# Seven half products for eight in the values and gates of two heads, and pauses moved behind the first eight pairs

## The chip, the core and the metric

The kernel runs on one core of a Trainium2 chip. The metric is the device time of one execution in microseconds (us). The kernel before takes 2068.49 us (median of 3 runs, 2067.83 to 2068.57).

## The reference, cut to what matters

Two layers over 256 tokens of 2048 columns, all in float32. Layer 0 is a gated linear attention with four heads, layer 1 a sliding-window attention, and each is followed by a squared-relu MLP of width 8192. The change touches two places: the values `v` and the gates `r` of the linear attention, and the order of the work in both MLPs.

```
u = rmsnorm(h, norm_mix[0])
proj = u @ w_in                       # (256, 2048) @ (2048, 6160)
q, k, v, r, glr = split(proj)         # v and r: 2048 columns each, 512 per head
o = gated_linear_attention(q, k, v, log_sigmoid(glr @ w_g2 + b_g) / 16)   # per head
o = rmsnorm(o, g_o) * silu(r)         # per head
h = h + o @ w_o
h = h + relu(rmsnorm(h, norm_mlp[0]) @ w1) ** 2 @ w2
```

## The kernel before

**Matmuls in two parts.** No operand is used as it is: each float32 matrix is split into a high part (rounded to the fast matmul type, `F32R`) and a low part (the rest), and a product is made of three matmuls, high x high, high x low and low x high. Weights come in tiles of 512 x 512 (four k-blocks of 128 rows, 1 MB) by a DMA of the SP queue. `halve` (line 104) splits one such tile in two halves: ScalarE (ACT) casts the high part (`wh`, line 116), VectorE (DVE) subtracts it for the low part (`wl`, line 117). `ws` and `wl` have three buffers, `wh` has four half buffers.

**Heads.** For each of the four heads, `gemm_mov` (line 138) is run twice over the four weight tiles of a column block of 512: once for the values (evacuated by `evac_v`, line 568) and once for the gates (`evac_r`, line 573, with the silu). The activations `act0` (16 k-blocks, high and low) stand still in the array and 512 weight columns move: per tile 4 k-blocks x 2 halves of the tokens x 3 parts = 24 matmuls of 512 columns, so 192 per head. The activations carry the norm's weight but not its factor `rstd`, which comes in at the evacuation. `mix_head` (line 562) joins a head's values and gates two to three ticks later, with a few full float32 matmuls and transposes on the tensor engine (PE).

**MLPs.** Each MLP runs four groups `g` (line 823). A group makes four wide products with `w1` (`gemm_wide`, line 192) and then multiplies their squared relu with a slab of `w2`: in `seven` (line 714, Strassen-Winograd on 2 x 2 half blocks in seven half products) for two column pairs, or, in the last group of the second MLP, by four more wide products. A wide product works in pairs: one matmul of 512 columns (high weights times high and low activations) and one of 256 (low weights times high), 16 pairs per weight tile and 64 per product, 256 per group. In its first tile the pairs of the first two of its four PSUM banks come first (the first eight pairs), then those of the other two.

**Pauses.** `pause` (line 678) issues two matmuls of one column each into a bank of tag `ms`; what they compute is not used. The first group of each MLP has two of them (at ticks 9 and 13 of the MLP), every later group one ahead of its first wide product, and the last wide stage of the second MLP one.

**Order of the work.** A helper `later(n, fn)` calls `fn` at the n-th `tick` from now; `gemm_mov`, `gemm_wide` and `seven` tick once for each half weight tile. Behind that, the framework orders the instructions of each engine when the kernel is built: by priority (the order of the program, with a head start for weight loads and splits), each as soon as its operands and buffers are free by the framework's own reckoning; an instruction that is not ready is passed by the next one that is. On the chip every engine then works through its list in that order. PSUM has eight banks: four of tag `acc`, two `tp`, two `ms`.

Of the kernel before, what the change touches and what calls it, by code (L numbers as in the profile page):

```python
# [16 lines left out]
P = 128  # L17
T = 256
NT = T // P
D = 2048  # L20
KT = D // P
C = 512
# [4 lines left out]
DV = 512  # L27
# [6 lines left out]
WS = 3  # L34
WHL = 4
WPRI = 60
# [4 lines left out]
RS = 4  # L41
# [7 lines left out]
def yoco_kernel(ctx: ExitStack, tc: tile.TileContext, x, norms, mlp_w1, mlp_w2, a_w_in, w_glr, w_gate, a_g_o, a_w_o,  # L49
                kv_w_k, kv_w_v, kv_g_k, b_w_q, b_g_q, b_sinks, b_w_o, out):  # L50
    nc = tc.nc
# [3 lines left out]
    actp = ctx.enter_context(tc.tile_pool(name="actp", bufs=8))  # L55
    wp = ctx.enter_context(tc.tile_pool(name="wp", bufs=2))
# [5 lines left out]
    def bank(shape, tag, dtype=F32):  # L62
        return ps[tag].tile(shape, dtype, name=tag, tag=tag)
# [29 lines left out]
    G_MIX0, G_MIX1, G_MLP0, G_MLP1, G_KV = (gT[:, KT * i:KT * (i + 1)] for i in range(5))  # L93
# [10 lines left out]
    def halve(ws, o=C, n=2, between=None):  # L104

        whs = [wp.tile([P, 2, C], F32R, name="wh", tag="wh", bufs=WHL) for _ in range(2)]
        wl = wp.tile([P, 4, C], F32R, name="wl", tag="wl", bufs=WS)
        with tc.high_priority(offset=WPRI):
            for k in range(0, 4, n):
                wh = whs[k // 2]  # L110
                js, ks = slice(k % 2, k % 2 + n), slice(k, k + n)
                with ExitStack() as order:
                    if between:
                        for ins in between(k):
                            order.enter_context(tc.issue_after(ins.ins))
                    h = nc.scalar.copy(out=wh[:, js, :o], in_=ws[:, ks, :o])  # L116
                    l = nc.vector.tensor_sub(out=wl[:, ks, :o], in0=ws[:, ks, :o], in1=wh.bitcast(F32)[:, js, :o])  # L117
                if between:
                    last[:] = h, l
        return [(whs[k // 2][:, k % 2], wl[:, k]) for k in range(4)]  # L120
# [14 lines left out]
    def piece(w, col, n=C):  # L135
        return lambda kq: [w[kq * C:(kq + 1) * C, col:col + n]]

    def gemm_mov(src, act, evac, step=4):

        accs = []  # L140

        def run(kq):
            if kq == 0:
                accs.extend(bank([P, C], "acc") for _ in range(NT))
            halves = split_w(src(kq), step)
            ah, al, _ = act[kq]
            for k in range(4):
                wh, wl = halves[k]
                for t in reversed(range(NT)):
                    tt = slice(t * P, (t + 1) * P)  # L150
                    st, sp = kq == 0 and k == 0, kq == 3 and k == 3
                    mm(accs[t], ah[:, k, tt], wh, st, False, skip_group_check=True)
                    mm(accs[t], ah[:, k, tt], wl, False, False, skip_group_check=True)
                    mm(accs[t], al[:, k, tt], wh, False, sp, skip_group_check=True)
                if k == 1:
                    tick()
            tick()
            if kq == 3:
                for t in reversed(range(NT)):
                    evac(t, accs[t])  # L160
        return run
# [128 lines left out]
    rb = sm.tile([P, T], F32, name="rb", tag="rb")  # L290
    ga = ExitStack()
    gp = ga.enter_context(tc.tile_pool(name="gp", bufs=1))
    ss = gp.tile([P, 2, T], F32, name="ss")
    rbq = gp.tile([P, T], F32, name="rbq")
    rb4, rbq4 = (a.rearrange("p (o t n) -> p o t n", o=1, t=NT).broadcast_to([P, 2, NT, P]) for a in (rb, rbq))
    sqx = []

# [31 lines left out]
    g2 = ga.enter_context(tc.tile_pool(name="g2", bufs=2))  # L329


    cum = gp.tile([P, NT, P], F32, name="cum")
    nc.gpsimd.memset(cum, 1.0 / TAU)
    for t, sign in enumerate((1, -1)):
        nc.gpsimd.affine_select(out=cum[:, t], in_=cum[:, t], compare_op=ALU.is_ge, fill=0.0, base=0,
# [13 lines left out]
    go = gp.tile([P, DV], F32, name="go")  # L349
# [181 lines left out]
    def mix(h, t, act):  # L531
# [25 lines left out]

        later(MX, flip)

    acto = [None] * H  # L560

    def mix_head(h, t):
# [4 lines left out]
    for h in range(H):  # L567
        def evac_v(t, acc, h=h):
            v = g2.tile([P, DV], F32, name="v", tag="v", bufs=4)
            nc.scalar.activation(out=v, in_=acc, func=AF.Copy, scale=rstd[:, t:t + 1])  # L570
            vs[h, t] = v

        def evac_r(t, acc, h=h):
            g = g2.tile([P, DV], F32, name="g", tag="g", bufs=4)
            nc.scalar.activation(out=g, in_=acc, func=AF.Silu, scale=rstd[:, t:t + 1])
            nc.gpsimd.tensor_mul(out=g, in0=g, in1=go)
            gs[h, t] = g

        go_all(gemm_mov(piece(w_in, 2048 + h * C), act0, evac_v))
        go_all(gemm_mov(piece(w_in, 4096 + h * C), act0, evac_r))  # L580
        for t in range(NT):
            later(2 + t, lambda h=h, t=t: mix_head(h, t))

# [83 lines left out]
    def mlp(w1, w2, act, r, gains):  # L667
# [155 lines left out]
        for g in range(4):  # L823
            w = w2[g * D:(g + 1) * D]
            seven_of = 0 if g == 3 and not gains else 2
            us, op, uf = {}, None, {}
            if g:
                pause()
            else:
                for n in (RS + 5, RS + 9):  # L830
                    later(n, pause)
            for c in range(NC4):
                if c >= seven_of:
                    us[c] = new_act()
# [24 lines left out]
                go_all(gemm_wide(piece(w1, g * D + c * C), act, evac_u))  # L859
            if seven_of:  # L860
                for n in range(2):
                    seven(w, n, op, us, g, g == 3 or (g == 2 and not gains), acts, gains if g == 3 else (), sq, nr)
                continue
            pause()
            for c in range(NC4):
                def evac_x(f, acc, c=c):
                    d = xt[c][:, f]
                    for u in (1, 0):
                        nc.vector.tensor_add(out=d, in0=acc[:, u], in1=d)
                    r = c * C + f * P  # L870
# [242 lines left out]
```

## Time and profile before

| | |
|---|---|
| median of 3 runs | 2068.49 us |
| the profiled execution | 2068.05 us, its span 2066.3 us |
| PE busy | 2053.9 us (99% of the span), 10778 matmuls |
| PE weight loads busy | 1743.0 us (84%) |
| DVE busy | 1429.5 us (69%) |
| ACT busy | 1151.7 us (56%) |
| GpSimd (POOL) busy | 159.0 us (8%) |
| granted PE clock, mean | 0.999 of full speed |
| HBM read | 406.71 MB, 198 GB/s over the span |

One execution was recorded by the hardware profiler. Busy time is the union of an engine's instructions; the records of matmuls overlap, since they are pipelined and their ends are modelled, so the pace of PE is read from the starts of its instructions or from their number in a stretch. Times of a row are us from the start of the span, durations of one instruction in ns where they say mean. An arrow `out<-in` names the tiles, `L117` is line 117 of the kernel.

### The profile page before, as it was taken

What the parts mean: (1) busy time and instruction counts of PE and PEld (TensorE: products, weight loads), DVE (VectorE), ACT (ScalarE), POOL (GpSimd) and SP (SyncE); (2) the same over time, 40 slices, a digit from 0 to 9 for tenths busy, and PEclk for the clock granted to TensorE, in tenths of its full rate; (3) what the DMA queues carried; (4) which work ended last, traced back from release to release, by engine and by line L of the source; (5) the groups of instructions that cost most, each with busy time, mean ns of one, the idle gap of its engine ahead of it and who ended that gap; (6) DMA issues with size and microseconds to landing.
All of it is one profiled execution on the core that took longest, in us unless ns stands there. A gap on an engine that the chain in (4) does not pass through costs nothing.

```text
span 2066.3 us, 27059 instructions
## 1 busy us (share of the span) xinstructions
PE 2053.9 (99%) x10778; PEld 1743.0 (84%) x10778; DVE 1429.5 (69%) x1632; ACT 1151.7 (56%) x1560; POOL 159.0 (8%) x171
## 2 busy tenths in 40 slices
PE   9999999999999999999999999999999999999999
PEld 9998888888888888888887877788888888888888
DVE  6686444567866886786798677666876786797554
ACT  6745445555555555554566677555655554655543
POOL 2252111000000000000001121000000000000000
PEclk9999999999999999999999999999999999999999
DMA  7445554755875785686676443655785776586653
GB/s 281 143 143 169 178 183 164 243 183 176 257 232 185 219 264 189 197 259 213 183 214 186 164 142 123 231 177 190 223 261 188 219 241 210 180 237 192 198 183 128
DMA packets 210654, 410.55 MB, mean 199 GB/s; under 512 B 7024, under 2 KB 15232, under 8 KB 210528
## 3 DMA queue, kind: packets, MB, share of 16 engines
q1 hardware_dynamic: 194704, 377.51, 53.9%
q0 software_dynamic: 15104, 30.23, 8.4%
q8 instruction: 84, 1.38, 0.3%
q10 hardware_dynamic: 720, 1.09, 0.2%
q14 instruction: 42, 0.34, 0.0%
HBM read 406.71 MB, written 2.10 MB: 198 GB/s over the span
## 4 chain that ended last, share of the span: by engine, by line
PE 94%; DVE 3%; ACT 2%; issue 1%; DMA 1%; POOL 0%; SPq 0%; ACTq 0%; DVEq 0%; POOLq 0%
PE acc L80 57%; PE ms L80 21%; PE tp L80 14%; ACT sc L1006 1%; DVE wl L117 1%; PE tp L606 1%; ACT wh L116 1%; DVE sc L1011 0%; PE tp L939 0%; DMA ws<-in_a_w_in_dram 0%; DVE st L1000 0%; DMA xt<-in_x_dram 0%; PE tp L555 0%; DVE po L1028 0%; DVE act L238 0%
## 5 line engine op out<-in xcount | busy, mean ns | idle before, releaser
L117 DVE TENSOR_TENSOR wl<-ws,wh 128x1024 fp32r<-128x1024 f32 (+1 forms) x636 | 778.8, 1232 | 455.4 <-ACT wh L116 453.2
L116 ACT CAST wh<-ws 128x1024 fp32r<-128x1024 f32 (+1 forms) x636 | 659.1, 1040 | 564.1 <-PE acc L80 372.1
L80 PE MATMUL acc<-wh,act 128*128 128x512 f32 x1792 | 574.5, 394 | 0.2 <-ACT act L237 0.2
L80 PE MATMUL acc<-act,wh 128*128 128x512 f32 (+1 forms) x1664 | 505.9, 365 | 2.1 <-ACT wh L116 1.3
L80 PEld LDWEIGHTS acc<-wh,act 128*128 128x128 f32 x1792 | 335.6, 188 | 72.4 <-issue 2.0
L80 PE MATMUL acc<-act,wl 128*128 128x256 f32 x1408 | 394.9, 281 | 0.2 <-DVE wl L117 0.2
L80 PE MATMUL acc<-wl,act 128*128 128x512 f32 x896 | 349.0, 390 | 0.0
L80 PEld LDWEIGHTS acc<-act,wh 128*128 128x128 f32 x1664 | 298.1, 190 | 54.2 <-ACT wh L116 1.5
L80 PEld LDWEIGHTS acc<-act,wl 128*128 128x128 f32 x1408 | 267.2, 190 | 1.4 <-DVE wl L117 0.5
L80 PE MATMUL tp<-act,wh 128*128 128x512 f32 x592 | 232.4, 397 | 0.0
L80 PE MATMUL ms<-act,wh 128*128 128x512 f32 x576 | 228.6, 397 | 0.0
L80 PEld LDWEIGHTS acc<-wl,act 128*128 128x128 f32 x896 | 168.4, 188 | 34.4 <-issue 1.7
L117 DVE TENSOR_TENSOR wl<-wx,wh 128x1024 fp32r<-128x1024 f32 x112 | 134.9, 1222 | 65.5 <-ACT wh L116 64.0
L116 ACT CAST wh<-wx 128x1024 fp32r<-128x1024 f32 x112 | 117.2, 1053 | 99.4 <-PE acc L80 42.3
L80 PE MATMUL ms<-act,wl 128*128 128x256 f32 x576 | 161.4, 280 | 0.0
L80 PE MATMUL tp<-act,wl 128*128 128x256 f32 x576 | 161.1, 280 | 0.0
L80 PE MATMUL ms<-wh,act 128*128 128x512 f32 x448 | 142.7, 390 | 0.0
L80 PEld LDWEIGHTS tp<-act,wh 128*128 128x128 f32 x592 | 111.1, 188 | 26.9
L80 PEld LDWEIGHTS ms<-act,wh 128*128 128x128 f32 x576 | 108.1, 188 | 26.3
L732 POOL DMA_DIRECT2D wx<-in_mlp_w_dram x28 | 36.1, 1290 | 1118.8 <-DVE wl L117 1017.8
L80 PEld LDWEIGHTS ms<-act,wl 128*128 128x128 f32 x576 | 108.7, 189 | 0.0
L80 PEld LDWEIGHTS tp<-act,wl 128*128 128x128 f32 x576 | 108.7, 189 | 0.0
(233 smaller groups left out, 2238.6 us busy)
## 6 DMA issues: line engine op xcount, KB each, us to landing
ws<-in_mlp_w_dram SPq DMA_DIRECT2D x228, 1024.0 KB, 5.2
ws<-in_a_w_in_dram SPq DMA_DIRECT2D x44, 1024.0 KB, 5.0
wx<-in_mlp_w_dram POOLq DMA_DIRECT2D x28, 1024.0 KB, 9.3
ws<-in_a_w_o_dram SPq DMA_DIRECT2D x16, 1024.0 KB, 4.9
ws<-in_b_w_q_dram SPq DMA_DIRECT2D x16, 1024.0 KB, 5.0
ws<-in_b_w_o_dram SPq DMA_DIRECT2D x16, 1024.0 KB, 5.0
wx<-in_mlp_w_dram SPq DMA_DIRECT2D x14, 1024.0 KB, 5.1
wy<-in_mlp_w_dram SPq DMA_DIRECT2D x14, 1024.0 KB, 8.0
```

The lines of the kernel that those rows point to most:

```text
L80: nc.tensor.matmul(o, lhsT=l, rhs=r, start=start, stop=stop, **kw)
L116: h = nc.scalar.copy(out=wh[:, js, :o], in_=ws[:, ks, :o])
L117: l = nc.vector.tensor_sub(out=wl[:, ks, :o], in0=ws[:, ks, :o], in1=wh.bitcast(F32)[:, js, :o])
L606: nc.tensor.transpose(out=tp[:, j, t], in_=xs[c][:, t, (2 * b + j) * P:(2 * b + j + 1) * P], identity=ident)
L732: nc.gpsimd.dma_start(out=ws, in_=block(i, j).rearrange("(k p) n -> p k n", p=P), accum_op=ALU.add)
L1006: nc.scalar.activation(out=sc[:, h], in_=sc[:, h], func=AF.Exp, bias=nmx[:, h:h + 1], scale=f[:, h:h + 1], accum_out=su[:, h:h + 1])
```

## The change

In heads 2 and 3 the eight weight tiles (four for the values, four for the gates) are no longer taken as eight products with both halves of the tokens. The upper two k-tiles of 512 rows and the two column blocks (values, gates) form a 2 x 2 matrix of weight tiles, the two token halves and the two k-tiles a 2 x 2 matrix of activations, and `seven_vr` makes their product in seven half products of 12 matmuls; the two other k-tiles are multiplied as before (`plain`, four times 24 matmuls). For this

- `normed` makes, during head 1, activations that carry the whole norm (`rstd` too), splits them anew, and makes four combinations of the two first k-tiles with their own high and low parts;
- the weight combinations are made in `wx` (a pair of half tiles): GpSimd starts two DMAs that add a tile on top of it in memory (`accum_op`), and DVE adds a tile to `b12` and to `wx`;
- `wx` has one half in `wx0`, whose memory `ss`, `rbq` and `cum` have used before, and one in a buffer of tag `mlev`; a fourth combination lives in `wgh`, the third in the other `mlev` buffer;
- the evacuations are adds, subtractions and copies, with the silu on top.

In the MLPs the second pause of the first group goes, and every other one is called at the first tick of its first wide product (behind the first eight pairs), not ahead of it.

```diff
+    def normed(b, *cs):
+        bs = slice(2 * b, 2 * b + 2)
+        us = []
+        for c in cs:
+            if b == 0:
+                xh[c] = new_act()
+            u = g2.tile([P, 2, T], F32, name="xu", tag="oh")
+            for j in range(2):
+                kt = 2 * b + j
+                nc.vector.scalar_tensor_tensor(out=u[:, j], in0=xt[c][:, kt], scalar=G_MIX0[:, c * 4 + kt:c * 4 + kt + 1],
+                                               in1=rb, op0=ALU.mult, op1=ALU.mult)
+            ah, al, _ = xh[c]
+            nc.scalar.copy(out=ah[:, bs], in_=u)
+            nc.vector.tensor_sub(out=al[:, bs], in0=u, in1=ah.bitcast(F32)[:, bs])
+            us.append(u)
+        if cs[0]:
+            return
...
+        ua, ub = us
+        es, sf = (g2.tile([P, 2, 2, P], F32, name="xe", tag="ol") for _ in range(2))
+        sub = lambda o, i, j: nc.vector.tensor_sub(out=o, in0=i, in1=j)
+        sub(es[:, 0], ua[:, :, P:], ub[:, :, P:])
+        sub(es[:, 1], ua[:, :, :P], es[:, 0])
+        sub(sf[:, 0], ub[:, :, :P], es[:, 1])
+        sub(sf[:, 1], ua[:, :, :P], ua[:, :, P:])
+        for o, e in zip(comb["es"], (es[:, 0], es[:, 1], sf[:, 0], sf[:, 1])):
+            nc.scalar.copy(out=o[:, 0, bs], in_=e)
+            sub(o[:, 1, bs], e, o.bitcast(F32)[:, 0, bs])
+
+    def seven_vr(h):
...
+        def load_x(i, j, queue=nc.gpsimd, **kw):
+            with tc.high_priority(offset=WPRI):
+                for n in range(2):
+                    queue.dma_start(out=wx[n], in_=block(i, j)[:, 2 * n:2 * n + 2], **kw)
...
+        def product(b, o, ws):
+            p, st = use(b)
+            halves = halve(ws)
+            for k in range(4):
+                wh, wl = halves[k]
+                mm(p, o[0][:, k], wh, st and k == 0, False, skip_group_check=True)
+                mm(p, o[0][:, k], wl, False, False, skip_group_check=True)
+                mm(p, o[1][:, k], wh, False, k == 3, skip_group_check=True)
+            tick()
+            return p
...
+        wx = [wx0, g2.tile([P, 2, C], F32, name="wx1", tag="mlev")]
+        load_x(0, 0, nc.sync)
+        p = product("A", token(0, 0), wx)
+        load_x(0, 1, accum_op=ALU.add)
+        nc.scalar.mul(out=v, in_=p, mul=-1.0)
+        plain(2, 1, "E", "F")
+        y = load(1, 1)
+        product("E", s4, y)
+        b12 = load(0, 1)
+        with tc.high_priority(offset=WPRI):
+            nc.vector.tensor_add(out=b12, in0=b12, in1=y)
+        p = product("C", e7, b12)
+        nc.scalar.copy(out=x22, in_=p)
+        plain(3, 1, "E", "F")
+        p = product("D", e5, wx)
+        load_x(1, 1, accum_op=ALU.add)
+        nc.scalar.copy(out=x21, in_=p)
+        plain(2, 0, "A", "C")
+        plain(3, 0, "A", "C")
+        add(v, product("D", s2, wx), v)
+        add(x12, banks["E"], v)
+        silu(x12)
+        sub(x22, v, x22)
+        add(x22, banks["F"], x22)
+        silu(x22)
+        sub(x21, x21, v)
+        b21 = load(1, 0)
+        with tc.high_priority(offset=WPRI):
+            for n in range(2):
+                nc.vector.tensor_add(out=wx[n], in0=wx[n], in1=b21[:, 2 * n:2 * n + 2])
+        product("A", token(1, 0), b21)
+        nc.scalar.copy(out=x11, in_=banks["A"])
+        add(x21, product("C", token(1, 1), wx), x21)
...
-        go_all(gemm_mov(piece(w_in, 2048 + h * C), act0, evac_v))
-        go_all(gemm_mov(piece(w_in, 4096 + h * C), act0, evac_r))
+        if h < 2:
+            if h == 2 - 1:
+                for n, fn in ((6, (0, 0, 1)), (8, (1, 0, 1)), (11, (0, 2)), (12, (1, 2)), (13, (0, 3)), (14, (1, 3))):
+                    later(n, lambda fn=fn: normed(*fn))
+            go_all(gemm_mov(piece(w_in, 2048 + h * C), act0, evac_v))
+            go_all(gemm_mov(piece(w_in, 4096 + h * C), act0, evac_r))
+        else:
+            seven_vr(h)
...
-            if g:
-                pause()
-            else:
-                for n in (RS + 5, RS + 9):
-                    later(n, pause)
+            later(1 if g else RS + 5, pause)
...
-            pause()
+            later(1, pause)
```

## Rows read from the trace of the kernel before

**Rows 1.** The page: PE's busy time, its granted clock, the chain by engine.
```profile
PE 2053.9 (99%) x10778; PEld 1743.0 (84%) x10778; DVE 1429.5 (69%) x1632; ACT 1151.7 (56%) x1560; POOL 159.0 (8%) x171
...
PEclk9999999999999999999999999999999999999999
...
PE 94%; DVE 3%; ACT 2%; issue 1%; DMA 1%; POOL 0%; SPq 0%; ACTq 0%; DVEq 0%; POOLq 0%
```

**Rows 2.** Stretches, heads then `seven`: us, each engine's busy us, PEclk, DMA share, GB/s.
```profile
198.00:218.00 20.00, 20.00 (x90) 16.57 (x89) 9.27 (x8) 8.64 (x9) 0.00 (x0) 1.00 0.58 183
...
510.00:550.80 40.80, 40.80 (x181) 33.76 (x180) 35.67 (x36) 25.58 (x29) 1.29 (x1) 1.00 0.80 240
```

**Rows 3.** Line 575, gate evacuation, two per head: duration, first and last start.
```profile
L575 ACT ACTIVATE g<-acc,rstd x8: 683/690/692, 175.3 to 319.8; 128x512 f32<-128x512 f32 x8
```

**Rows 4.** Lines of 222 to 265 us, in the heads: the weight split on DVE.
```profile
L117 DVE TENSOR_TENSOR wl<-ws,wh 128x1024 fp32r<-128x1024 f32 x15 | 19.0, 1268 | 22.8 <-ACT wh L116 22.8
```

**Rows 5.** Lines of the whole span by form: DVE operations, count, busy us, mean ns.
```profile
L803 DVE TENSOR_TENSOR wy<-wy,ws 128x2048 f32<-128x2048 f32 x14 | 32.0, 2287 | 0.1
...
L238 DVE SCALAR_TENSOR_TENSOR act<-tp,gT,act 128x256 fp32r<-128x256 f32 x64 | 30.0, 480 | 9.4 <-ACT act L237 9.2
L846 DVE TENSOR_TENSOR m<-acc,m 128x256 f32<-128x256 f32 x64 | 24.7, 423 | 0.0
L855 DVE TENSOR_TENSOR act<-u,act 128x512 fp32r<-128x512 f32 x36 | 24.4, 683 | 0.0
...
L544 DVE SCALAR_TENSOR_TENSOR og<-ms,ov,g 128x512 f32<-128x512 f32 x8 | 6.0, 751 | 5.7 <-POOL ov L245 5.7
```

**Rows 6.** DVE in order of time while GpSimd works on levels beside it: start, us.
```profile
148.00 2.06 DVE L117 TENSOR_TENSOR wl<-ws,wh 128x1024 fp32r<-128x1024 f32 x1
```

**Rows 7.** DMA issues: KB each, median us to landing.
```profile
wx<-in_mlp_w_dram POOLq DMA_DIRECT2D x28, 1024.0 KB, 9.3
...
ws<-in_kv_w_k_dram SPq DMA_DIRECT2D x4, 512.0 KB, 4.5
```

**Rows 8.** Line 732, the adding DMAs in `seven`: issue on POOL in ns, us to landing.
```profile
L732 POOL DMA_DIRECT2D wx<-in_mlp_w_dram x28: 1274/1283/1375, 506.9 to 1852.9; - x28
...
DMA to landing us min/median/max: 8.4/9.3/12.0
```

**Rows 9.** DVE in order of time at the end of a `seven`: start, us.
```profile
587.48 1.22 DVE L117 TENSOR_TENSOR wl<-wx,wh 128x1024 fp32r<-128x1024 f32 x1
...
593.75 0.69 DVE L769 TENSOR_TENSOR xs<-acc,xs 128x512 f32<-128x512 f32 x1
```

**Rows 10.** Stretches inside wide products, columns as in Rows 2.
```profile
466.00:506.00 40.00, 40.00 (x228) 34.67 (x227) 26.45 (x33) 21.19 (x28) 0.00 (x0) 1.00 0.55 185
600.00:670.00 70.00, 70.00 (x398) 60.74 (x397) 45.75 (x56) 37.88 (x52) 0.00 (x0) 1.00 0.58 182
...
1890.00:1960.00 70.00, 70.00 (x406) 61.16 (x405) 41.76 (x50) 36.47 (x50) 0.00 (x0) 1.00 0.61 195
```

**Rows 11.** PE in order of time at the start of a group: start, us.
```profile
591.21 0.50 PE L80 MATMUL ms<-ones,ident 128*128 128x1 f32 x4
591.58 0.47 PE L80 MATMUL acc<-act,wh 128*128 128x512 f32 x1
...
592.01 0.40 PE L80 MATMUL acc<-act,wh 128*128 128x512 f32 x1
...
594.78 0.62 PE L80 MATMUL acc<-act,wh 128*128 128x512 f32 x2
595.25 0.40 PE L80 MATMUL acc<-act,wl 128*128 128x256 f32 x2
```

**Rows 12.** PE in order of time at the first MLP's second pause: start, us.
```profile
463.73 0.39 PE L80 MATMUL acc<-act,wh 128*128 128x512 f32 x1
...
464.12 0.60 PE L80 MATMUL ms<-ones,ident 128*128 128x1 f32 x4
464.59 0.48 PE L80 MATMUL acc<-act,wh 128*128 128x512 f32 x1
```

More of the change, by code (lines that the diff above doesn't have):

```diff
@@ L115, in halve @@
                             order.enter_context(tc.issue_after(ins.ins))
-                    h = nc.scalar.copy(out=wh[:, js, :o], in_=ws[:, ks, :o])
-                    l = nc.vector.tensor_sub(out=wl[:, ks, :o], in0=ws[:, ks, :o], in1=wh.bitcast(F32)[:, js, :o])
+                    w = ws[k // 2] if isinstance(ws, list) else ws[:, ks, :o]
+                    h = nc.scalar.copy(out=wh[:, js, :o], in_=w)
+                    l = nc.vector.tensor_sub(out=wl[:, ks, :o], in0=w, in1=wh.bitcast(F32)[:, js, :o])
                 if between:
@@ L292, in yoco_kernel @@
     gp = ga.enter_context(tc.tile_pool(name="gp", bufs=1))
-    ss = gp.tile([P, 2, T], F32, name="ss")
-    rbq = gp.tile([P, T], F32, name="rbq")
+    wx0 = gp.tile([P, 2, C], F32, name="wx0")
+    ss, rbq = wx0[:, 0].rearrange("p (a t) -> p a t", a=2), wx0[:, 1, :T]
     rb4, rbq4 = (a.rearrange("p (o t n) -> p o t n", o=1, t=NT).broadcast_to([P, 2, NT, P]) for a in (rb, rbq))
@@ L329, in yoco_kernel @@
     g2 = ga.enter_context(tc.tile_pool(name="g2", bufs=2))
-    cum = gp.tile([P, NT, P], F32, name="cum")
+    cum = wx0[:, 1, T:].rearrange("p (t n) -> p t n", t=NT)
     nc.gpsimd.memset(cum, 1.0 / TAU)
@@ L558, in mix @@
         later(MX, flip)
+    xh, comb = {}, {}
+    def normed(b, *cs):
[15 more added lines that the diff above has]
+            return
+        if b == 0:
+            pair = actp.tile([P, 2, 2, 4, P], F32R, name="cmb", tag="act")
+            comb["es"] = [pair[:, i] for i in range(2)] + \
+                [g2.tile([P, 2, 4, P], F32R, name="cmb1", tag="mlev"),
+                 wgh.rearrange("p (a k n) -> p a k n", a=2, k=4)]
+        ua, ub = us
[8 more added lines that the diff above has]
+            sub(o[:, 1, bs], e, o.bitcast(F32)[:, 0, bs])
@@ new lines, in seven_vr, with use, block, load @@
+    def seven_vr(h):
+        banks = {}
+        def use(b):
+            if b in banks:
+                return banks[b], False
+            banks[b] = bank([P, C], "tp" if b == "D" else "acc")
+            return banks[b], True
+        def block(i, j):
+            c = (2048, 4096)[j] + h * C
+            return w_in[i * C:(i + 1) * C, c:c + C].rearrange("(k p) n -> p k n", p=P)
+        def load(i, j):
+            ws = wp.tile([P, 4, C], F32, name="ws", tag="ws", bufs=WS)
+            with tc.high_priority(offset=WPRI):
+                nc.sync.dma_start(out=ws, in_=block(i, j))
+            return ws
+        def load_x(i, j, queue=nc.gpsimd, **kw):
+            with tc.high_priority(offset=WPRI):
+                for n in range(2):
+                    queue.dma_start(out=wx[n], in_=block(i, j)[:, 2 * n:2 * n + 2], **kw)
+        def token(c, t):
+            return [a[:, :, t * P:(t + 1) * P] for a in xh[c][:2]]
+        e5, s2, s4, e7 = ([o[:, 0], o[:, 1]] for o in comb["es"])
+        def product(b, o, ws):
[8 more added lines that the diff above has]
+            return p
+        def plain(i, j, b0, b1):
+            halves = halve(load(i, j))
+            ps_ = [use(b) for b in (b0, b1)]
+            for k in range(4):
+                wh, wl = halves[k]
+                for t in range(NT):
+                    p, st = ps_[t]
+                    a, l = token(i, t)
+                    mm(p, a[:, k], wh, st and k == 0, False, skip_group_check=True)
+                    mm(p, a[:, k], wl, False, False, skip_group_check=True)
+                    mm(p, l[:, k], wh, False, k == 3, skip_group_check=True)
+                if k % 2:
+                    tick()
+        add = lambda o, i, j: nc.vector.tensor_add(out=o, in0=i, in1=j)
+        sub = lambda o, i, j: nc.vector.tensor_sub(out=o, in0=i, in1=j)
+        v = g2.tile([P, C], F32, name="vp", tag="vp", bufs=1)
+        for t in range(NT):
+            vs[h, t] = g2.tile([P, DV], F32, name="v", tag="v", bufs=4)
+            gs[h, t] = g2.tile([P, DV], F32, name="g", tag="g", bufs=4)
+        x11, x21, x12, x22 = vs[h, 0], vs[h, 1], gs[h, 0], gs[h, 1]
+        def silu(g):
+            nc.scalar.activation(out=g, in_=g, func=AF.Silu)
+            nc.gpsimd.tensor_mul(out=g, in0=g, in1=go)
+        wx = [wx0, g2.tile([P, 2, C], F32, name="wx1", tag="mlev")]
[25 more added lines that the diff above has]
+        b21 = load(1, 0)
+        with tc.high_priority(offset=WPRI):
+            for n in range(2):
[3 more added lines that the diff above has]
+        add(x21, product("C", token(1, 1), wx), x21)
```

## The prediction

> **What bounds the kernel now.** I read the page first. PE is busy for 99% of the span, its granted clock is at full speed (the 2.4 GHz level) in all 40 slices, and 94% of the chain that ended last is PE [rows 1]. So time is won or lost in two ways only: by the number and the pace of PE's instructions, or by a stall that something else puts on PE. The second view, by stretches, gives the pace. In `seven` a stretch of 40.80 us holds 180 matmuls of 512 columns (one of the 181 straddles an edge), which is 0.2267 us for each [rows 2]; PE is without a gap although DVE is busy for 35.67 us of it. In the heads DVE is busy for only 9.27 of 20 us. The third view is the same one inside the wide products, and here the reader is to see something that a busy share hides: 70 us of the second group hold 398 matmuls, 70 us of the last group of the second MLP hold 406, the same instructions on the same tiles at the same clock [rows 10]. A pair takes 70/199 = 0.3518 us in the one and 70/203 = 0.3448 us in the other, so 0.007 us more, or 2%. The wide products have a slow and a fast gait.
>
> Where the gait comes from is seen in order of time. After the pause at 591.21 us PE starts at 591.58, and nine pairs later, at 594.78, two wide matmuls run one behind the other and then two narrow ones [rows 11]: the tenth pair was passed by a matmul of the eleventh, because the fourth bank was not yet given free in the framework's reckoning (its last reader is the DVE add at 593.75 [rows 9]). The eight pairs from 592.01 to there take 2.77/8 = 0.346 us each; the stretch behind it runs at 0.3518 to the end of the group. I read this as: a pause leaves PE in the fast gait, a disturbance leaves it in the slow one. Against this stands one pause, the second of the first MLP at 464.12: the 40 us behind it hold 228 matmuls, 40/114 = 0.351 us a pair, slow [rows 10, 12].
>
> **The change, part by part.** The sum is made against the profiled execution, 2068.05 us, which lies 0.44 us below the median of the runs.
>
> *Fewer matmuls.* Each of the heads 2 and 3 makes 7 x 12 + 4 x 24 = 180 matmuls for 192. 24 fewer at 0.2267 us: -5.44 us, all of it on the chain.
>
> *The activations of head 1 (`normed`).* DVE: 16 scaled multiplies of 256 columns at 0.480, 8 low parts of 512 at 0.683, 16 subtractions of 256 at 0.423 [rows 5]: 7.7 + 5.5 + 6.8 = 20.0 us. A head lasts (319.8 - 175.3)/3 = 48.2 us on average, by the last gate evacuations of heads 0 and 3 [rows 3]. From tick 6 of 16 some 30 us are left, and DVE is idle in (20 - 9.27)/20 = 54% of that: 16 us. So 4 us spill into head 2. Weight splits stand ahead of this work in priority, and one operation of it delays a split by 0.7 us at most, with two tiles in stock. Cost: nothing; if that cover is gone, the 4 us.
>
> *DVE in the heads 2 and 3.* 22 splits at 1.268 [rows 4], adds of 2048 columns at 2.287, of 2 x 1024 at about the same in total, 6 adds of 512 at 0.683, and two mixes of 0.751: 27.9 + 2.3 + 2.3 + 4.1 + 1.5 = 38.1 us. The head will last 48.2 - 2.7 = 45.5 us. So DVE has 84% of the time, less than in `seven` (35.67 of 40.80, 87%), where PE has no gap [rows 2]. Cost: nothing.
>
> *The transfers that add.* They are issued behind the split of `wx` for the first D product and must be split again by the second, which starts 12 + 48 = 60 matmuls, 13.6 us, behind the first. If that split ends only with the start of its product, as the last one of a `seven` does [rows 9], it takes 1.28 us for the issue and 9.3 us to the landing [rows 8], then a cast and a subtraction, each taken as 1.27 us [rows 4]: 13.1 us, just in time. With the longest landing, 12.0 us, it is 2.2 us late in each head. Splits run further ahead than that where ACT and DVE have room, so I take nothing, with +4.4 us as the upper end for both heads. What is queued on POOL behind a waiting issue is a mix or a gate, for which only later transposes and the mix wait.
>
> *The first load of head 3.* `wx` has one buffer. Its last reading in head 2 is the split for the last product; in `seven` that split ends at 588.70 us [rows 9], 0.2 us behind the start of its product (12 matmuls ahead of 591.21 [rows 11]). Then 512 KB take 4.5 us by the nearest row [rows 7], cast and subtraction 2.5 us: 7.2 us, where PE wants the weights 2.7 us after the start of that product. So 4.5 us are uncovered at most. At best none are: the 24 matmuls of `plain(2, 1)` (5.4 us) need no `wx` and can pass in the framework's order. On SP the other weight loads stand behind this one only if the framework leaves them there; it passes them by the same rule. I take 1.0 us, near the lower end, because a matmul that isn't ready is passed elsewhere in this trace [rows 11], and 0.2 us for the start of head 2.
>
> Heads together: -5.44 + 1.2 = -4.2 us (from -5.4 to +3.5, with all of these waits in full: 4.5 + 4.4).
>
> *Two pauses fewer.* From the start of the pair at 463.73 to that of the next at 464.59 it takes 0.86 us for 0.35 [rows 12]; 0.51 us for each of two, -1.0 us.
>
> *The gait of the first MLP's first group.* Without the pause at 464 the fast gait should last: 127 pairs x 0.007 us, -0.9 us (from -0.9 to 0). In the second MLP that group is taken as fast already.
>
> *The pauses behind the first eight pairs.* They cost what they cost ahead of them. The groups 1 to 3 of the first MLP and 1 and 2 of the second have the disturbance and then the slow gait for some 247 pairs: 247 x 0.007 = 1.7 us each, five times -8.5 us if the pause now stands where it sets the gait for the rest, nothing if not, and up to +1.7 us each in the two fast groups of the second MLP if it sets the slow one there. The trace shows no pause in that place, and its two nearest rows say different things: a pause is followed by the fast gait [rows 11], the disturbance by the slow one. The program's order puts the pause one pair ahead of the matmul that was passed. I take -8.5, because the pause shifts the tenth pair in the framework's reckoning, where the bank was missing for less than the one matmul that was moved up (0.23 us), while a pause is worth some 0.4 us; if it no longer has to wait, nothing is left to disturb. That is a choice and not a working. The last wide stage of the second MLP is broken off by transposes in its first ticks, with the pause or without: nothing, from -1.7 to 0. The eight pairs ahead of it run in the slow gait then: six groups x 8 x 0.007 = +0.3 us.
>
> Sum: -4.2 - 1.0 - 0.9 - 8.5 + 0.3 = -14.3 us: 2053.75 for the profiled execution, 2054.2 against the median, so **2054 us**.
>
> One rule speaks against the heads. In the stretch where POOL works on levels beside DVE a split takes 2.06 us [rows 6] for 1.27 in the heads. The Trainium skill (SBUF — State Buffer, "Who interferes with whom") says that a DVE instruction with both inputs in SBUF and a GpSimd instruction that reads SBUF block each other for whole instructions. The trace agrees as far as that row goes. By it the splits of the heads, which have POOL's gates and low parts beside them, would stretch; this is the mechanism of the rival on the slower side.
>
> **The rivals.**
>
> *The slow gait stays.* The tenth pair is still passed, one pair behind the pause, and the five groups stay slow. For it: the pause takes as long behind the eight pairs as ahead of them, so the tenth pair comes at the same time, and all five groups show the same disturbance. Against it: the margin is under 0.23 us. Then -8.5 goes: 2068.5 - 5.8 = 2062.7, so 2062 to 2063 us.
>
> *The heads give nothing and the gait stays.* The load of `wx` is not covered and costs its 4.5 us, with 0.2 us at the start of head 2: heads -0.7; with -1.0, -0.9 and +0.3 the sum is -2.3: 2066.2 us. For it: one buffer where `seven` has two. Against it: other matmuls are ready.
>
> *DVE bounds the heads, slower than before.* DVE has 38.1 us of 45.5; if each of the 22 splits took 2.06 us as beside POOL, it would have 38.1 + 22 x 0.79 = 55.5 us, 10 us more than the head, in two heads +20 us. With -5.44 and -1.6 for the rest: about 2081 us. It decides from a mean split of 1.27 + 7.4/22 = 1.61 us on, and brings a loss from about 1.77 us on. Against it: POOL's operations per head stay the same, and there the split's mean is 1.268 [rows 4].
>
> **How the numbers follow.** Fast gait behind the pauses, 2054 us: 0.46. Slow gait stays, 2062.5: 0.33. The heads give nothing, 2066: 0.13. DVE bounds the heads: 0.08. About 0.2% (4.1 us) is what a measurement of this kernel can tell from no change, so faster begins below 2064.4 us. The first two cases are faster nearly throughout, the third is the same: faster 0.78, same 0.14, slower 0.08. Range: the low end is the first case with no wait in the heads and rounding of the gait's gain by 2 us, 2050.5; the high end takes in the third case, 2066.5. Left out are the fourth case and the tails.
>
> **What would show it.** 180 matmuls per head in 40.8 us of PE time and no gap above 1 us at the start of head 3 in order of time. 203 pairs in 70 us of the groups 1 to 3 of the first MLP; 199 there would be the second case. No two wide matmuls in a row at the tenth pair. DVE in heads 2 and 3 at some 84%, its split at 1.27 us. If the heads show PE waiting for `wl` (DVE) or `wh` (ACT), or if the last group of the second MLP falls to 398 matmuls in 70 us, the prediction is wrong in that part.

## The result, and the profile after

The changed kernel takes 2057.24 us, the median of five runs (2057.00 to 2058.51), against 2068.14 us for the kernel before on the same chip. The ratio is 0.9949, with a 95% interval from 0.9935 to 0.9963: 10.9 us faster. The forecast was 2054 us with a range from 2050.5 to 2066.5. The time is in the range, but two of the reasons behind it were wrong, and the runs show which.

The page of the kernel after, the lines that answer to [rows 1]:

```profile
PE 2040.6 (99%) x10746; PEld 1734.5 (84%) x10746; DVE 1478.4 (72%) x1702; ACT 1171.5 (57%) x1592; POOL 172.2 (8%) x179
...
PE 92%; DVE 4%; ACT 2%; DMA 1%; issue 1%; SPq 0%; POOL 0%; ACTq 0%; DVEq 0%; POOLq 0%
```

PE has 32 instructions fewer (24 of the products, and 8 of two pauses, each of which stands in the trace as four one-column matmuls). PE's share of the chain fell from 94% to 92%, and DVE's rose from 3% to 4%; DMA's is 1% in both. Somewhere PE may now wait. Where, and at what pace it runs elsewhere, is seen in stretches of the kernel after (us, each engine's busy us with its instructions, PEclk, DMA share, GB/s). The first two answer to [rows 10], the rest to the heads in [rows 2]:

```profile
466.00:500.00 34.00, 34.00 (x197) 29.98 (x197) 24.73 (x32) 19.87 (x28) 0.00 (x0) 1.00 0.56 187
600.00:670.00 70.00, 70.00 (x407) 61.22 (x405) 45.89 (x56) 38.54 (x53) 0.00 (x0) 1.00 0.59 191
...
175.00:220.00 45.00, 45.00 (x208) 36.44 (x207) 38.28 (x62) 30.57 (x47) 8.18 (x7) 1.00 0.60 194
220.00:265.00 45.00, 45.00 (x203) 36.25 (x203) 32.75 (x28) 27.68 (x35) 11.40 (x10) 1.00 0.73 193
265.00:310.00 45.00, 42.20 (x181) 33.22 (x181) 34.81 (x33) 27.45 (x36) 14.13 (x10) 0.96 0.79 232
...
269.00:272.00 3.00, 2.02 (x6) 0.66 (x4) 2.27 (x2) 1.64 (x3) 2.81 (x2) 1.00 0.62 231
272.00:275.00 3.00, 1.18 (x4) 0.78 (x5) 2.97 (x4) 3.00 (x6) 1.62 (x2) 1.00 0.00 0
275.00:279.00 4.00, 4.00 (x12) 3.12 (x11) 4.00 (x4) 1.50 (x2) 1.95 (x2) 0.57 0.62 93
279.00:290.00 11.00, 11.00 (x53) 8.74 (x51) 6.64 (x9) 8.09 (x12) 3.01 (x4) 1.00 1.03 314
```

The gait is there: 407 matmuls in 70 us of the second group, where 398 stood before. The heads are not: in the 45 us from 265 to 310 PE is idle for 2.80 us, all of it between 269 and 275, at the start of head 3. What that costs is read from the starts of the matmuls below. Four full float32 matmuls of the mix begin at 269.14 and take 0.43 us each, as they do in the kernel before, so the next one was due at 270.86. It starts at 272.09, 1.2 us late, and the one behind it, due 0.23 us later, at 274.31, another 2.0 us late. From there to the start at 279.00 PE starts 13 matmuls in 4.69 us, which at 0.2267 us each would take 2.95: 1.7 us more, in which PE hardly stands but the granted clock is 0.57 (275 to 279 us), a mean of the 1.2 and the 2.4 GHz level. Together 5.0 us are lost.

What it waits for, in order of time (start, us, engine, line, output and inputs; in brackets the idle time and its releaser):

```profile
264.91 2.10 SPq L623 DMA_DIRECT2D wx<-in_a_w_in_dram  x2
...
267.97 1.60 POOL L665 TENSOR_TENSOR g<-g,go 128x512 f32<-128x512 f32 x1 [22.16 <-ACT g L664]
...
269.14 1.88 PE L80 MATMUL ms<-v,AT 128*128 128x512 f32 x4
...
269.75 2.29 DVE L678 TENSOR_TENSOR ws<-ws 128x2048 f32<-128x2048 f32 x1 [0.73 <-DMA ws<-in_a_w_in_dram]
269.76 3.41 POOL L665 TENSOR_TENSOR g<-g,go 128x512 f32<-128x512 f32 x1 [0.19 <-ACT g L664]
...
270.99 1.05 ACT L117 CAST wh<-wx 128x1024 fp32r<-128x1024 f32 x1 [1.30 <-DMA wx<-in_a_w_in_dram]
...
272.07 2.19 DVE L118 TENSOR_TENSOR wl<-wx,wh 128x1024 fp32r<-128x1024 f32 x1
...
272.09 0.49 PE L80 MATMUL acc<-wh,act 128*128 128x512 f32 x1 [1.07 <-ACT wh L117]
...
273.46 2.00 ACT L117 CAST wh<-ws 128x1024 fp32r<-128x1024 f32 x2
...
274.31 0.50 PE L80 MATMUL acc<-wl,act 128*128 128x512 f32 x1 [1.73 <-DVE wl L118]
...
275.36 1.83 PE L80 MATMUL acc<-wh,act 128*128 128x512 f32 x4
...
279.00 0.39 PE L80 MATMUL acc<-wl,act 128*128 128x512 f32 x1
```

This is the load of `wx` for the first product of head 3. It is issued at 264.91, as soon as the first half of `wx` is free. ACT, which has `wx` next in its list, waits for it until 270.99; the casts of the weights of `plain(2, 1)` stand behind in the same list and come at 273.46, although their tile was in memory (the tile for the sum of line 678, which is loaded behind it, had landed by 269.75). On DVE the sum for the third product (line 678) keeps the engine busy until 272.04, which is when the cast of `wx` ends (270.99 + 1.05), so by itself it delays the split by next to nothing. Then the split takes 2.19 us for 1.2. From the issue to the first product's second matmul it is 9.4 us, for 4.5 + 2.5 = 7.0 in the forecast, and after the four matmuls of the mix no matmul of another product passes in between.

The four instructions from 269.75 to 274.26 are worth reading closely. Gate multiplies of this shape take 1.29 us at the shortest in the kernel before (line 576); the one at 267.97 takes 1.60. The one at 269.76, begun 0.01 us behind the add, takes 3.41 and ends at 273.17, 1.13 us behind the end of the add (272.04). The split, begun at 272.07, ends 1.09 us after that multiply, and a split with nothing beside it takes 1.22 (the mean for `wx` from 222 to 265 us). So, to within 0.2 us, each stood until the other had ended. This is what the Trainium skill says (SBUF — State Buffer, "Who interferes with whom"): a DVE instruction with both inputs in SBUF and a GpSimd instruction that reads SBUF lock each other out for the whole instruction. The trace agrees to that measure. By this reading the sum of line 678 costs the split its microsecond by way of POOL, whose multiply it pushed into the split; no run moved the sum.

### The profile page after: what moved, and what is told of

Same layout as the page of the kernel before. It is cut to its first block, busy times and chain, and to the rows that moved or that the text cites. A ratio compares the mean times of both kernels' runs of the same rounds, so it can differ in the third digit from the quotient of the medians.

```text
span 2056.8 us, 27147 instructions
## 1 busy us (share of the span) xinstructions
PE 2040.6 (99%) x10746; PEld 1734.5 (84%) x10746; DVE 1478.4 (72%) x1702; ACT 1171.5 (57%) x1592; POOL 172.2 (8%) x179
## 3 DMA queue, kind: packets, MB, share of 16 engines
q10 hardware_dynamic: 720, 1.09, 0.2%
## 4 chain that ended last, share of the span: by engine, by line
PE 92%; DVE 4%; ACT 2%; DMA 1%; issue 1%; SPq 0%; POOL 0%; ACTq 0%; DVEq 0%; POOLq 0%
PE acc L80 56%; PE ms L80 21%; PE tp L80 14%; DVE wl L118 1%; ACT sc L1150 1%; PE tp L754 1%; ACT wh L117 1%; DVE sc L1155 0%; DMA xt<-in_x_dram 0%; PE tp L1083 0%; DVE st L1144 0%; DMA ws<-in_a_w_in_dram 0%; DMA wx<-in_a_w_in_dram 0%; PE tp L557 0%; DVE po L1172 0%
## 5 line engine op out<-in xcount | busy, mean ns | idle before, releaser
L80 PE MATMUL acc<-wh,act 128*128 128x512 f32 x1712 | 549.7, 395 | 1.2 <-ACT wh L117 1.1
L80 PEld LDWEIGHTS acc<-wh,act 128*128 128x128 f32 x1712 | 321.3, 188 | 70.7 <-ACT wh L117 2.1
L80 PE MATMUL acc<-wl,act 128*128 128x512 f32 x856 | 334.0, 390 | 1.7 <-DVE wl L118 1.7
L118 DVE TENSOR_TENSOR wl<-wx,wh 128x1024 fp32r<-128x1024 f32 x128 | 155.4, 1230 | 69.2 <-ACT wh L117 67.3
L117 ACT CAST wh<-wx 128x1024 fp32r<-128x1024 f32 x128 | 134.1, 1054 | 110.3 <-PE acc L80 53.0
L80 PEld LDWEIGHTS acc<-wl,act 128*128 128x128 f32 x856 | 161.3, 188 | 34.5 <-DVE wl L118 2.3
```

The costliest lines, as they stand in the source:

```text
L117: h = nc.scalar.copy(out=wh[:, js, :o], in_=w)
L118: l = nc.vector.tensor_sub(out=wl[:, ks, :o], in0=w, in1=wh.bitcast(F32)[:, js, :o])
```

## The experiments

Each ran in five rounds beside the kernel before (2068.23 us in the first series, 2068.84 and 2068.86 in the later two). What the heads bring by themselves is read from the time between the last gate evacuation of head 1 and the first matmul of the first wide product: 192.76 us before (224.53 to 417.29), 192.99 after (225.36 to 418.35). The same time is 192.73 in `e1_pauses_only`, whose heads are unchanged (225.09 to 417.82), and 193.06 in `e2_heads_only`, whose heads are changed (225.11 to 418.17). So the heads cost 0.2 us, where the fewer matmuls alone were to save 5.44: 5.7 us are lost.

**Which half of the change it is.** `e1_pauses_only` is the kernel before with the edit of the pauses alone, `e2_heads_only` that of the heads alone. (In the code here and below, statements of two lines are joined.)

```
 e1:
-            if g: pause()
-            else: for n in (RS + 5, RS + 9): later(n, pause)
+            later(1 if g else RS + 5, pause)
...
-            pause()                 # the last wide stage
+            later(1, pause)
```

> The kernel before with the change of the pauses alone. Theory (the gain is the gait of the wide products, -10.4 us in the sum, and the heads bring next to nothing): 2068.1 - 10.4 = 2057.7 us, with 405 to 406 matmuls in 70 us of each of the groups that had 398. Rival (half and half: the pauses give only part of it and the heads the rest, as in the sum on record, -4.2): 2061 to 2063 us.

> The kernel before with the seven half products in heads 2 and 3 alone. Theory (the 5.4 us saved are spent at the start of head 3, where PE waits some 3 us for wx and then runs some 4 us at the lower clock): 2067.0 to 2068.0 us, the same as before within the measurement, with a stretch of PE idle in head 3. Rival (the heads bring the 4.2 us of the sum on record): 2064 us. Groups 1 to 3 of the first MLP stay at 398 matmuls in 70 us in both.

e1 took 2058.18 us, ratio 0.9951 (0.9939 to 0.9964): -10.05 us. e2 took 2068.37 us, ratio 1.0000 (0.9992 to 1.0009): nothing. Stretches of e1, then of e2:

```profile
600.00:670.00 70.00, 70.00 (x405) 61.23 (x404) 46.28 (x57) 38.09 (x53) 0.00 (x0) 1.00 0.59 194
```

```profile
600.00:670.00 70.00, 70.00 (x398) 60.75 (x397) 45.38 (x57) 37.88 (x52) 0.00 (x0) 1.00 0.56 182
...
269.00:272.00 3.00, 1.77 (x5) 0.46 (x3) 2.34 (x1) 1.53 (x3) 1.58 (x2) 1.00 0.59 214
272.00:275.00 3.00, 1.39 (x3) 0.98 (x4) 3.00 (x4) 3.00 (x5) 0.64 (x1) 0.86 0.00 0
275.00:279.00 4.00, 4.00 (x13) 3.13 (x13) 4.00 (x4) 1.42 (x3) 1.75 (x2) 0.68 0.72 99
```

The whole gain is the pauses', and the wait at head 3 is the heads' own.

**Whether the load of `wx` is the wait.** Three edits of the changed kernel. `e3_swap_last` swaps the last two products of `seven_vr`, so that `wx` is free one product earlier; `e5_plain_first` gives PE other work ahead; `e6_ring_for_A` takes the first weights of head 3 from the ring of `ws`, and `wx` is off the path.

```
 e3:
+        add(x21, product("C", token(1, 1), wx), x21)
         product("A", token(1, 0), b21)
         nc.scalar.copy(out=x11, in_=banks["A"])
-        add(x21, product("C", token(1, 1), wx), x21)
 e5:
+        plain(2, 1, "E", "F")
         p = product("A", token(0, 0), wx)
         load_x(0, 1, accum_op=ALU.add)
         nc.scalar.mul(out=v, in_=p, mul=-1.0)
-        plain(2, 1, "E", "F")
 e6:
+        if h == 3: p = product("A", token(0, 0), load(0, 0))
         load_x(0, 0, nc.sync)
+        if h == 2: p = product("A", token(0, 0), wx)
-        p = product("A", token(0, 0), wx)
```

> The changed kernel with the last two products of a head in the other order: the one that reads wx comes first, then the one that reads b21, so wx comes free one product (2.7 us) earlier. Theory (the wait of head 3 is the reload of the single wx buffer, and the lower clock is its consequence): the idle time falls from 3.2 us to 0.5 us or less, the clock stays at its full level, and the time falls by 4 to 5 us to 2052.5 to 2053.5 us. Rival (DVE or ACT, full at that place, holds the first product of head 3): the wait stays at 2 us or more, 2056 to 2057 us.

> The changed kernel with plain(2, 1) ahead of product A in heads 2 and 3, so that 24 matmuls (5.4 us) that do not need wx stand between the end of head 2 and the first reading of wx. Theory (the reload of wx is what PE waits for; other ready matmuls would cover it, as the sum on record assumed): PE idle at the start of head 3 falls below 1 us, the clock stays, 2052.5 to 2054 us. Rival (DVE is full there: adds for b12, splits and the end of head 2 stand in one queue, and ws buffers run short, as in the run with the last products swapped): the wait moves to the splits of plain(2, 1) or of E, 2056 to 2059 us.

> The changed kernel where the first product of head 3 takes its weights from the ring of ws buffers; wx is loaded beside it and is needed only at the first D product (1 MB more is read). Theory (reload of wx): PE's wait at the start of head 3 goes, 2052.5 to 2054 us. Rival (DVE and the three ws buffers bound the passage from head 2 to head 3, whichever buffer is used): PE still waits 2 us or more between 266 and 290 us, 2056 us or more.

e3 took 2058.72 us (ratio 0.9951, 0.9938 to 0.9965): no gain over the changed kernel, and the theory missed. e5 took 2054.69 us (0.9933, 0.9920 to 0.9947), e6 2056.50 us (0.9943, 0.9931 to 0.9956). By the mark above the heads give e5 -3.0 us (224.90 to 414.62), e6 -1.7 (225.00 to 416.06), e3 +1.2 (224.94 to 418.88). Stretches of e3:

```profile
272.00:275.00 3.00, 2.52 (x9) 1.43 (x8) 3.00 (x3) 2.04 (x3) 1.93 (x2) 1.00 0.68 111
275.00:279.00 4.00, 3.27 (x14) 2.74 (x15) 4.00 (x5) 1.80 (x4) 2.13 (x1) 1.00 1.01 226
279.00:290.00 11.00, 9.21 (x37) 6.59 (x36) 8.66 (x10) 7.15 (x11) 4.31 (x4) 0.91 0.71 242
```

and its two longer waits on PE (start, us, in brackets the idle time and its releaser), with what runs on DVE and POOL ahead of the second:

```profile
275.74 0.50 PE L80 MATMUL acc<-wh,act 128*128 128x512 f32 x1 [1.02 <-DVE g L655]
...
283.32 2.35 DVE L118 TENSOR_TENSOR wl<-ws,wh 128x1024 fp32r<-128x1024 f32 x2
...
284.56 2.24 POOL L550 TENSOR_TENSOR ol<-og,oh 128x512 fp32r<-128x512 f32 x1 [1.94 <-ACT oh L549]
...
286.85 0.53 PE L557 MATMUL tp<-identr,ol 128*128 128x128 f32 x4 [1.78 <-POOL ol L550]
```

Stretches of e6:

```profile
272.00:275.00 3.00, 2.52 (x10) 1.45 (x9) 3.00 (x5) 2.01 (x4) 1.79 (x2) 1.00 1.05 266
275.00:279.00 4.00, 4.00 (x19) 3.13 (x18) 4.00 (x4) 0.55 (x2) 1.53 (x1) 1.00 1.07 277
279.00:290.00 11.00, 9.21 (x47) 6.69 (x46) 8.66 (x10) 8.59 (x13) 4.68 (x4) 1.00 0.88 262
```

and its two waits on PE:

```profile
274.36 0.50 PE L80 MATMUL acc<-wh,act 128*128 128x512 f32 x1 [0.48 <-DVE g L655]
...
285.47 0.53 PE L557 MATMUL tp<-identr,ol 128*128 128x128 f32 x4 [1.79 <-POOL ol L550]
```

Stretches of e5:

```profile
269.00:272.00 3.00, 3.00 (x15) 2.49 (x14) 3.00 (x5) 1.08 (x2) 1.19 (x1) 1.00 0.96 332
272.00:275.00 3.00, 3.00 (x14) 2.12 (x12) 3.00 (x3) 3.00 (x4) 2.31 (x2) 1.00 0.52 203
275.00:279.00 4.00, 4.00 (x16) 2.82 (x15) 4.00 (x4) 1.26 (x4) 1.58 (x2) 1.00 0.77 114
279.00:290.00 11.00, 9.78 (x51) 7.45 (x49) 10.28 (x11) 10.30 (x16) 5.64 (x5) 1.00 0.85 253
```

and the longer of its two waits on PE (0.69 and 0.53 us):

```profile
283.57 0.53 PE L557 MATMUL tp<-identr,oh 128*128 128x128 f32 x4 [0.69 <-ACT oh L549]
```

With `wx` off the path other waits take its place. In e3 and e6 PE waits first for an add on PSUM (line 655) that stands behind splits, while DVE is busy for all of 272 to 279 us. Then it waits longer, 1.78 and 1.79 us, for POOL's low part of the mix (line 550). That step takes 2.24 us in both runs, where the same step takes 1.28 to 1.30 in all heads of the kernel before; in e3 it ends 1.13 us after the splits beside it (285.67), as the gate multiply did above. Over 269 to 290 us PE is idle for 3.1 us in e3 and 2.3 in e6, so both came out on the side of their rivals, and e3 loses at the clock again (0.91). In e5 DVE is busy for 20.28 of 21 us from 269 to 290, and PE still waits 1.22 us, later, for the mix's ACT and POOL steps; its time lies 0.7 us above its theory's range. So there are two limits at the change of heads: the load, which e5 covers, and behind it DVE and POOL, where the epilogue of one head, the first sums of the next and the splits fall together. A second buffer for `wx`, which would take the load away without moving a product, was not tried, and no run shows whether SBUF has room for it.

**What sets the gait.** The forecast took the passed pair for the disturbance, and the slow gait for what it leaves. PE at the start of the second group of the kernel after, to be set beside [rows 11]:

```profile
593.62 0.50 PE L80 MATMUL ms<-ones,ident 128*128 128x1 f32 x4
593.98 0.48 PE L80 MATMUL acc<-act,wh 128*128 128x512 f32 x1
...
594.41 0.63 PE L80 MATMUL acc<-act,wh 128*128 128x512 f32 x2
594.88 0.40 PE L80 MATMUL acc<-act,wl 128*128 128x256 f32 x2
```

The passed pair is the one with two wide matmuls in a row (x2). It is still passed, one pair behind the pause, and yet the gait behind it is fast. Five runs vary the pause and the passed pair; three of them come first. `e4_order_pause_ahead` is the kernel before with its pauses where they were, and the order of the first tiles changed so that none has to wait for the fourth bank; in `e7_no_pause` all pauses are gone; `e8_pause_behind_4` is e1 with the pause of the later groups behind the first four pairs.

```
 e4:
-  order = [(k, 2 * h + f) for h in range(2) for k in range(4) for f in range(2)]
+  order = ([(k, f) for k in range(4) for f in range(2)]
+           + [(k, 2 + f) for f in range(2) for k in range(4)])
 e7:
-            if g: pause()
-            else: for n in (RS + 5, RS + 9): later(n, pause)
...
-            pause()
 e8, in the wide loop:
+                if i == 3 and early: early.pop()()
 and
-            later(1 if g else RS + 5, pause)
+            if g: early.append(pause)
+            else: later(RS + 5, pause)
```

> The kernel before, pauses where they were, but in the first tile of each wide product the pairs of the fourth bank come behind all four of the third, so that no matmul is passed there and the pairs follow each other regularly behind the pause. Theory A (two wide matmuls in a row, nine pairs behind the pause, set the slow gait in five groups): those five groups run at 405 to 406 matmuls in 70 us, 5 x 1.7 = 8.5 us less, 2059.6 us. Theory B (the gait is set by something else, say the distance from the last product of seven to the pause): the groups stay at 398, 2068 us.

> The kernel before without any pause. Theory (wide products fall into the slow gait behind the regular stream of seven and behind transposes, and only a pause brings the fast one): all groups at 397 to 399 matmuls in 70 us, also the last group of the second MLP, which had 406; eleven pauses less are worth about -5.1 us, the gait of that group and of the first group of the second MLP costs +2.6 us: 2065.5 us. Rival (the gait is a matter of the order alone, without the disturbance of a pause the products run fast): 2055 to 2058 us.

> The changed pauses alone, but behind the first four pairs in the later groups: the matmul that is passed now comes five pairs behind the pause, where it came one pair behind it with the pause behind eight pairs (fast gait) and nine behind it with the pause ahead (slow gait). Theory A (a disturbance directly behind a pause does no harm, since the weight loads are still far ahead, and one that comes later does): slow gait in five groups, 2066 to 2067 us. Theory B (the pause must only stand inside the wide product, not between two kinds of streams): fast gait, 2058 us.

e4 took 2060.13 us (0.9962, 0.9950 to 0.9975), e8 2066.24 us (0.9989, 0.9980 to 0.9997), both as their theory A had it. e7 took 2058.47 us (0.9950, 0.9938 to 0.9963), with single runs from 2055.51 to 2061.87; the theory that only a pause brings the fast gait (2065.5) fell. A stretch of the second group of e4, of e8, and of e7 with its second MLP's first group:

```profile
600.00:670.00 70.00, 70.00 (x406) 61.20 (x406) 46.37 (x57) 38.29 (x53) 0.00 (x0) 1.00 0.58 187
```

```profile
600.00:670.00 70.00, 70.00 (x398) 60.67 (x398) 46.04 (x56) 37.20 (x53) 0.00 (x0) 1.00 0.58 188
```

```profile
600.00:670.00 70.00, 70.00 (x405) 61.22 (x404) 46.34 (x57) 37.87 (x52) 0.00 (x0) 1.00 0.59 192
1365.00:1435.00 70.00, 70.00 (x399) 60.73 (x399) 45.18 (x56) 38.14 (x53) 0.00 (x0) 1.00 0.58 186
```

**Both together.** `e9_plain_first_group_pause` is e5 with the pauses in the first group of each MLP alone, seven fewer. `e10_no_passed_pair` has e4's order as well, so that in the later groups there is neither a pause nor a passed pair.

```
 e9, e10:
-            later(1 if g else RS + 5, pause)
+            if g == 0:
+                later(RS + 5, pause)
...
-            later(1, pause)
```

> The changed kernel with plain(2, 1) ahead of the first D product in heads 2 and 3, and pauses in the first group of each MLP only (7 of 9 pauses gone). Theory A (the passed pair switches the gait only where a pause is near ahead of it, and switches slow to fast where none is; between groups the gait is carried on): groups 1 to 3 of the first MLP come out of a fast group and meet a passed pair with no pause ahead: what it does to a fast gait without a pause has been seen only in the kernel without pauses, where groups stayed fast. Then 2054.7 - 7 x 0.45 = 2051.5 us. Rival (a passed pair throws a fast gait into the slow one wherever no pause stands one pair ahead): five groups slow, + 8.5: 2060 us.

> As e9_plain_first_group_pause, and the first two tiles' pairs of the fourth bank behind all four of the third, so that no pair is passed. Theory A (only the passed pair switches the gait): the fast gait of the first group's pause is carried through the groups: 2051.5 us. Rival (the change of stage itself ends the fast gait, so each group needs its own pause): groups 1 to 3 slow from their start, about 2060 us.

e9 took 2054.80 us (0.9934, 0.9921 to 0.9948), with single runs from 2051.38 to 2056.56; e10 2061.77 us (0.9964, 0.9952 to 0.9977). The median of e9 met neither value of its expectation: theory A's 2051.5 is its fastest run, and the rival's 2060 was not reached. The profiled run of e9 is its fastest, as is that of e7. PE around the passed pair of its second group:

```profile
589.47 0.28 PE L80 MATMUL acc<-act,wl 128*128 128x256 f32 x1
589.59 0.40 PE L80 MATMUL acc<-act,wh 128*128 128x512 f32 x1
...
589.95 0.62 PE L80 MATMUL acc<-act,wh 128*128 128x512 f32 x2
590.41 0.40 PE L80 MATMUL acc<-act,wl 128*128 128x256 f32 x2
```

A stretch behind it, then the same stretch of e10:

```profile
600.00:670.00 70.00, 70.00 (x406) 61.21 (x405) 46.21 (x57) 37.86 (x52) 0.00 (x0) 1.00 0.58 188
```

```profile
600.00:670.00 70.00, 70.00 (x398) 60.67 (x397) 45.76 (x56) 37.80 (x52) 0.00 (x0) 1.00 0.57 182
```

The two differ in the passed pair alone, and by six groups at 398 or 406 matmuls: six times 1.7 us less seven pauses is 6.9 us over e5, and 7.1 were measured. So a later group without a pause and without a passed pair begins in the slow gait and keeps it (e10); e10's theory A, that the gait is carried from group to group, fell. The runs together:

| start of a later group | runs | gait of the rest |
|---|---|---|
| no pause, no passed pair | e10 | slow |
| pause ahead, no passed pair | e4 | fast |
| pause ahead, passed pair 9 pairs behind it | before, e2 | slow in the first MLP and two groups of the second |
| pause, passed pair 5 pairs behind it | e8 | slow in the same five groups |
| pause, passed pair one pair behind it | after, e1, e3, e5, e6 | fast |
| no pause, passed pair | e7, e9 | fast in the profiled run; the times spread over 5 to 6 us |

So a pause ahead of a later group takes PE into the fast gait (e4 against e10) and a passed pair can take it out of it (before against e4); a passed pair out of the slow gait can also take it into the fast one (e9 against e10). Neither does so everywhere. The second pause of the first MLP leaves the slow gait behind it [rows 10, 12], and without it the gait there stays fast (197 matmuls from 466 to 500 us, where the kernel before has 194). In the last group of the second MLP a wide matmul is moved up too, 12 pairs behind the pause before and 4 after, and the gait is fast in both; there the second narrow matmul comes 11 pairs later, not at once. What in PE carries the gait is open: no view read here shows it. Open too is whether the pause of the kernel after brings the fast gait or only makes the passed pair behind it do so each time; its runs lie within 1.5 us where those without spread over 5 to 6, which is three groups at 1.7 us. That the slow groups in the slower runs of e7 and e9 make this spread is inferred, since one run of each was profiled.

The best version is e5: 14.2 us faster than the kernel before in its series, where the changed kernel was 10.9 us faster in its own, so some 3.3 us better; the mark gives the same (-3.0 against +0.2). e9 has the fastest single run but the same median.

## Why the prediction was right or wrong

- *Fewer matmuls, -5.44 us:* right as a count. It was spent by what the next point tells.
- *The first load of head 3, 1.0 us (1.2 with the start of head 2):* **the step that failed**. By the mark 5.7 us were lost, 5.0 of them at head 3; where the other 0.7 lie was not traced. PE fell behind by 3.2 us waiting, which is inside the bound of 4.5, and then by 1.7 us at the lower clock, for which the sum had no term. I chose the lower end because a matmul that isn't ready is passed elsewhere [rows 11]. PE's matmuls of `plain(2, 1)` could pass; their weights could not, because ACT's casts and DVE's splits stand in lists of their own, in which `wx` was ahead. The load took 6.1 us to the cast for 4.5, and the split was stretched by 1.0 us.
- *The adding transfers, nothing:* right. Their median landing here is 7.0 us, and PE is without a gap in the windows around them except the one above. *normed, nothing:* right, PE 45.00 of 45.00 us from 175 to 220.
- *DVE in the heads, 84% and splits of 1.27 us:* the share is lower, 32.75 and 34.81 of 45 us (73% and 77%), the splits take 1.33 us on average for tiles in `ws` and 1.29 for those in `wx`. (The length of a head, 48.2 us, was misread: [rows 3] gives the first start in head 0 and the last in head 3, two per head. From first to first, 175.31 to 318.21, it is 47.6, which changes no term of the sum.) The argument from the mean was the mistake: over 269 to 279 us DVE is busy for 9.24 of 10. The rival in which DVE bounds the heads had the mechanism in part, at one place and for a microsecond, not over two heads.
- *The rival in which the heads give nothing* was right on the heads (-0.7 by its sum, +0.2 by the mark, both close to nothing) and wrong on the gait, with which I had tied it.
- *Two pauses fewer, -1.0 us:* a pause is worth 0.47 us: the profiled runs of e5 and e9, with the fast gait in both, differ by 3.28 us for seven. *The first group, -0.9, and five groups, -8.5, less 0.3 for the slow pairs ahead:* -10.1 with the two pauses, -10.05 in e1. The size came from the counts of matmuls in equal stretches and held.
- *Why the gait changes* was wrong in its ground: "no two wide matmuls in a row at the tenth pair" was the sign named, and they are there. In these five groups the distance between pause and passed pair decides (fast at one pair, slow at five and nine), which no row before showed. The -8.5 was put down as a choice and not a working, and that it came out is luck as far as the reason given for it goes.

With 5.7 us in place of 1.2 the sum is -9.8 us, within the measured interval (-13.4 to -7.7).

## What to carry to other kernels

When work is taken off the engine that bounds, look at the next start of a stage with one buffer, and follow its load through every list it passes: a matmul may be ready and its cast may stand behind one that isn't. An engine's mean share says nothing of the ten microseconds in which two stages overlap. Count instructions in equal stretches of equal work: a pace that differs by 2% is invisible in busy shares and was worth more here than 24 matmuls.

## What the runs showed that I had not expected

- The same pairs of a 512 and a 256 column matmul run at 0.352 or 0.345 us for a whole stage (398 or 406 in 70 us), at the same granted clock; four one-column matmuls, or two pairs in another order, change it.
- Where PE had been idle for 2.80 of 6 us, the granted clock was 0.57 in the four behind and 1.00 in the stretch after those: the wait cost 1.7 us beyond its own length. In e5, whose waits at head 3 are shorter (0.69 and 0.53 us), it stayed at 1.00.
- In e3 and e6 a low part on POOL (line 550) takes 2.24 us for 1.29 beside DVE's splits, and PE waits 1.8 us for it: POOL, busy for a twelfth of the span, is on the path there.
